# Tiles of normed activations and of the feed-forward's inner values, 32 bytes longer per partition

## The chip, the cores and the metric

The kernel runs on one core of a Trainium2 chip. The metric is the device time of one execution in microseconds. Five engines work side by side and meet at semaphores: TensorE (PE in the rows, with its weight loads as PEld), VectorE (DVE), ScalarE (ACT), GpSimd (POOL) and SyncE (SP, which here only issues transfers).

## What is computed

A two-layer diffusion-style transformer block followed by a second block with a mixer, on one sequence of 512 tokens with 1024 features, all in float32. Cut to the lines that hold nearly all of the arithmetic:

```python
def conv_ffn(hn, win, conv_w, conv_b, wout):      # twice: 1024 -> 2 x 2816 -> 1024
    u = hn @ win
    y = conv_b + sum(up[:, tap:tap + S] * conv_w[tap] for tap in range(3))
    gate, val = jnp.split(y, 2, axis=-1)
    return (jax.nn.silu(gate) * val) @ wout

def swiglu(u, w_gate, w_up, w_down):              # twice: 1024 -> 2 x 2816 -> 1024
    return (jax.nn.silu(u @ w_gate) * (u @ w_up)) @ w_down
...
# between them: attention over chunks with a relative bias (16 heads), latent attention (16 heads),
# and a mixer of differential attention (8 heads) and an mLSTM (4 heads); every branch starts from
# modulate(rms_norm(h)) and ends with h = h + gate * (o @ w_out)
```

## The kernel before

**How a product is made.** Activations lie with features on the 128 partitions and the 512 tokens along the free axis, in tiles of 128 x 512 float32. A product keeps float32's precision by splitting each operand into an upper part H (type float32r) and a remainder L, and by adding three products: H·H, H·L, L·H. `mm3` (L325) issues them on L327, L328 and L329: the weight block (128 x 128) is the stationary operand, the activations (128 x 512) are the moving one, in the order H, L, H. `gemm` (L331) runs `mm3` over the 8 feature tiles: 24 matmuls into one PSUM tile `ps_g`. Weight slabs come by DMA into `wr` and are split by ScalarE (L310) and VectorE (L311) into `wh` and `wl`.

**The tiles that are touched.** `hl` (L343) makes a pair (H, L) of such activations. With the tag `u`, in the pool `gp`, it makes the normed and modulated activations of every branch (8 pairs), the heads' outputs on their way to an output product, and the latents. With the tag `hid`, in the pool `pf`, it makes the inner values of the feed forward. A tag has a fixed number of buffers, which its tiles take in turn: 16 for `u`, 24 for `hid`. In a pool, the buffers of a tag lie one behind the other. Each is 2048 bytes per partition, so in the kernel before all 16 buffers of `u` begin at the same place within 128 bytes. In the built program that place is 64 (the first buffer begins at byte 69312 = 541 x 128 + 64). The weights' buffers `wh` and `wl` (4096 bytes each) all begin at 64, too. The buffers of `hid` begin at 64 in the first convolutional feed forward (where a pool with two tiles of one column is open beneath `pf`), and at 0 in the other three. The tile `xs` (mLSTM's convolved inputs) begins at 0, the tile `yh` (outputs of the differential attention) at 64, the tiles `tw` (weights for the last two row blocks of a branch) at 0 in the first attention and at 64 in the latent attention. The trace shows no addresses: these are read from the built program.

**The order of the work.** The program is one long sequence written out at build time, with the semaphores set from the tiles' uses: attention (to 300 us), first convolutional feed forward (300 to 690), latent attention (690 to 960), second convolutional feed forward (960 to 1340), first gated feed forward (1340 to 1715), mixer (1715 to 2290), second gated feed forward (from 2290). A feed forward runs in three parts of 8, 8 and 4 inner tiles: two `gemm` from `u` for each inner tile, split into `hid`, then 8 output columns from `hid`, `n` inner tiles each. The last two inner tiles are multiplied in halves of 256 tokens (`tail`, L430), so that the next norm can begin on the first half.

Of the kernel before, what the change touches and what calls it, by code (L numbers as in the profile page):

```python
# [31 lines left out]

# ---------------------------------------------------------------- layout

# [35 lines left out]
def _tail(w):  # L70
    """last TAIL row blocks: [2][128][4 column blocks x TAIL x 128]"""
    return _group(_blocks(w[-TAIL * P:]), 4)
# [111 lines left out]

# ---------------------------------------------------------------- device

# [5 lines left out]
class _Norm:  # L192
    """Norm of the residual stream and its modulation, by columns of tokens."""

# [33 lines left out]
class _Norm2(_Norm):  # L228
    """Final norm of the first block (gain g), then the norm that the second block starts with.

    With A the sum of h**2 and B that of (g h)**2 over the D features, the product of the two factors
    (A / D + EPS) ** -0.5 and (B / D / (A / D + EPS) + EPS) ** -0.5 is ((B + EPS A) / D + EPS ** 2) ** -0.5.
    """

# [23 lines left out]
    def finish(self):  # L258
        """the residual stream itself after the first of the two norms"""
        k, nc = self.k, self.k.nc  # L260
        for cs in HALVES:
            k.rsqrt(self.r1, self.sums(cs), D, cs, self.t)
        for j in range(KD):
            h = k.h[j]
            nc.vector.scalar_tensor_tensor(h, h, self.g[:, j:j + 1], self.r1, ALU.mult, ALU.mult)


class _NormOut(_Norm):
    """Final norm, to memory."""

# [13 lines left out]
class _K:  # L284
# [8 lines left out]

    # ---- small helpers
    def col(self, name, j=0, n=1):
# [18 lines left out]
    def stream(self, specs, ahead=1):  # L314
        """wload(*spec) for each, as many ahead of their use"""
        q = [self.wload(*specs.pop(0)) for _ in range(ahead)]

        def take():
            if specs:
                q.append(self.wload(*specs.pop(0)))  # L320
            return q.pop(0)

        return take
# [19 lines left out]
    def hl(self, pool, tag, bufs, src=None):  # L343
        h = pool.tile([P, T], F32R, tag=tag, bufs=bufs, name=tag + "h")
        l = pool.tile([P, T], F32R, tag=tag, bufs=bufs, name=tag + "l")
        if src is not None:
            self.split(src, h, l)
        return h, l
# [4 lines left out]

    # ---- norms: sums of squares over the features, by columns of tokens
    def sq(self, acc, j, src, cs=FULL, scale=1.0, eng=None, first=False):
# [14 lines left out]
    def lnexp(self, ins):  # L370
        """the table set that has both Ln and Exp, loaded behind ins"""
        with self.tc.issue_after(ins.ins):
            self.preload = self.nc.scalar.preload_act_table_set("natural_log_exp_and_others")

    def rsqrt(self, r, ms, dim, cs, tmp, eps=None):
        """r = (ms / dim + EPS) ** -0.5; with eps, that constant (its tile, its value) for EPS"""
        nc = self.nc
        r, t = r[:, cs], tmp[:, cs]
        with self.tc.issue_after(self.preload.ins):
            nc.scalar.activation(r, ms, AF.Ln, bias=eps[0] if eps else self.eps, scale=1.0 / dim)  # L380
            nc.scalar.activation(r, r, AF.Exp, scale=-0.5)
        nc.vector.scalar_tensor_tensor(t, r, -0.5 / dim, r, ALU.mult, ALU.mult)
        nc.vector.scalar_tensor_tensor(t, ms, (eps[1] if eps else EPS) * dim, t, ALU.add, ALU.mult)
        nc.vector.scalar_tensor_tensor(r, t, 1.5, r, ALU.add, ALU.mult)
# [33 lines left out]

    # ---- last products of a branch by halves of the tokens, each followed by its half of the next norm
    def tail_weights(self, pool, tags, wname):  # L420
        """(H, L) for each half of the column blocks"""
        nc = self.nc
        w = [pool.tile([P, 1024], F32R, tag=t, bufs=n, name="tw") for t, n in tags]
        for q in range(2):
            r = self.gp.tile([P, 1024], F32, tag="wr", bufs=4, name="wr")
            nc.sync.dma_start(r, self.a[wname][q])
            self.split(r, w[2 * q], w[2 * q + 1])
        return w
# [17 lines left out]
    def gemm_halves(self, ws, acts):  # L446
        """column blocks ws (H, L) on the first tokens, then on the others"""
        pss = [self.pg() for _ in ws]
# [6 lines left out]

    # ---- modulation vectors: one column of 128 outputs per job
    def gemv(self, j, cact, bias):
# [11 lines left out]

    # ---- attention of one head: softmax per tile of queries, block transposes, values  # L470
    def softmax(self, pool, s, n, add, scale, pn):
        """exp((s+add)*scale - max) and, in st, 1/sum at column 2."""
        nc = self.nc
# [7 lines left out]
    def heads(self, pool, n, begin, lag=2):  # L481
        """n heads, a tile of queries at a time; transposes run lag tiles behind the softmax.

        begin(h) -> probs, v, m, done: probs(i) gives the normalized [128 queries, 128(i+1) keys], v the values
        (H, L), [128 keys, 4, m], done takes the result, [m, 512]."""
        wait = []
# [18 lines left out]
    def transpose(self, i, p, pt):  # L505
        """query tile i of the probabilities into the upper and lower parts, keys on partitions"""
        t = self.pg(tag="t")
# [13 lines left out]
    def stacked(self, src, tiles, keys, scale=1.0):  # L521
        """Rows 64 e on of src as two operands e for products over 128 rows.

        tiles: three; the first two become the operands, with the upper part in rows 64 e on and the lower part
        in the other rows, or for keys the upper part in all; the third gets the lower parts, rows as in src."""
        nc = self.nc
# [9 lines left out]
    def stacked_scores(self, s, q, k, low, e, i, stop=True):  # L536
        """scores of query tile i with the keys up to its end"""
        nc = self.nc
        rs, qs, ks = slice(64 * e, 64 * e + 64), slice(i * P, i * P + P), slice(0, i * P + P)
        nc.tensor.matmul(s, q[:, qs], k[:, ks], start=True, stop=False)  # L540
        nc.tensor.matmul(s, q[rs, qs], low[rs, ks], start=False, stop=stop)  # L541
# [7 lines left out]
    def pair_out(self, pool, dram, p, ps, e):  # L549
        """output of head 2p+e into the rows of its pair; pairs but the last wait in DRAM."""  # L550
        if e == 0:
# [15 lines left out]

    # ---- program
    def build(self):
# [44 lines left out]
    def c_act(self, ca, j):  # L614
        """silu of a row of c on every partition"""
        nc = self.nc
# [21 lines left out]

    # ---- first layer: attention over chunks with relative bias
    def block_a(self, cact, m0):  # L640
# [85 lines left out]
    def branch_out(self, pool, tags, od, w, gate, mk_norm):  # L726
        """product of the heads' outputs with the output weights, into the residual stream"""
        tw = self.tail_weights(pool, tags, w + "t")
# [7 lines left out]

    # ---- feed forward with a causal convolution
    def conv_ffn(self, l, norm, gate, nbg, mk_norm):
# [45 lines left out]

    # ---- second layer: latent attention
    def rope(self, pool, ps, cos, sin):
# [127 lines left out]

    # ---- gated feed forward
    def swiglu(self, n, norm, gt, mk_norm):
# [18 lines left out]

    # ---- second block's mixer
    def mix(self, norm, ada):
# [100 lines left out]
    def ml_gates(self, pp, gps, plc, slr, b):  # L1038
        """gate pre-activations to the exponents of the quadratic form, relative to chunks."""
        nc, a = self.nc, self.a  # L1040
# [52 lines left out]
    def ml_heads(self, pl, u, mg, dram, plc, tri, slr, b):  # L1093
# [7 lines left out]
        def back4(n, h):  # L1101
            """H and L of the two blocks of a head, as split"""
            t = pl.tile([P, 4, T], F32R, tag="xs", bufs=4, name=n)
# [8 lines left out]
        def scores(h):  # L1112
            """weighted scores, keys on partitions: (H, L) of the queries from 128 j on for each tile j of keys"""
            ksl, qsl = back4("mk", h), back4("mq", h)
# [48 lines left out]
        def normed(h, num, den):  # L1163
            """with d the greater of |den| and exp(em), the norm of num / d is
            num * (mean(num ** 2) + EPS * d ** 2) ** -0.5; acc sums to 256 times what is in brackets"""
            em = self.pg()
# [56 lines left out]
    def diff(self, u, px):  # L1223
# [3 lines left out]
        with self.tc.tile_pool(name="pd", bufs=1) as pd:  # L1227
# [11 lines left out]
            nc.scalar.activation(lc[:, 0:2], lc[:, 0:2], AF.Exp)  # L1239
            # -(exp(a) - exp(b) + 0.2)  # L1240
            nc.vector.tensor_tensor(lc[:, 2:3], lc[:, 1:2], lc[:, 0:1], ALU.subtract)
# [94 lines left out]
```

## Time and profile before

| what | value |
|---|---|
| median of the runs shown (2767.37, 2770.97) | 2769.17 us |
| span of the profiled execution | 2771.6 us |
| TensorE busy | 2659.2 us, 96% |
| TensorE weight loads | 2129.6 us, 77% |
| VectorE busy | 1759.9 us, 63% |
| ScalarE busy | 1205.0 us, 43% |
| granted TensorE clock, mean | 0.980 of 2.4 GHz |

The profile has one execution's time, its span; it is 2.4 us over the median of the runs. A matmul's duration in the rows is longer than its share of the engine, because matmuls are pipelined: one is still draining while the next streams. What a matmul costs in a stream is the distance from its start to the next one's start (its pace). The timeline rows give starts with two decimals, so the pace is taken over many matmuls.

### The profile page before, as it was taken

The page shows a single profiled execution, that of the slowest core. Times are in us where ns is not written, and L with a number is a line of the kernel's source. Part 1 is how long each engine was busy: PE and PEld are TensorE (multiplying, and loading weights), DVE is VectorE, ACT ScalarE, POOL GpSimd, SP SyncE. Part 2 cuts the span into 40 slices and gives each one's busy share as a digit, 9 for nine tenths or more (in the row PEclk, how much of TensorE's full clock was granted, in tenths as well). Part 3 has the DMA queues.
Part 4 walks back from the last instruction along what each step waited for, and adds up shares of the span by engine and source line. Part 5 has one row for each costly group of instructions (what it writes and reads, how often), then busy time and mean ns, then how long its engine had stood idle before and what let it go on. Part 6 is the DMA issues. An engine that isn't in the chain of part 4 may idle for free.

```text
span 2771.6 us, 33871 instructions
## 1 busy us (share of the span) xinstructions
PE 2659.2 (96%) x12306; PEld 2129.6 (77%) x12306; DVE 1759.9 (63%) x3349; ACT 1205.0 (43%) x2100; POOL 91.8 (3%) x138
## 2 busy tenths in 40 slices
PE   7999899999899999999899999999999999999997
PEld 5777778788677778878788888777777777788886
DVE  7777896866778896966733335788456456533334
ACT  5565532334567442324522223566446334422222
POOL 1000200000000100000100001000000000100000
PEclk9999999999899999999999999999999999999999
DMA  8664476652143475753133332322247754233331
GB/s 271 188 184 144 145 248 204 223 173 79 43 106 111 139 229 187 252 176 120 54 99 93 98 113 80 92 75 78 72 149 258 239 186 133 77 95 95 99 107 46
DMA packets 138092, 385.24 MB, mean 139 GB/s; under 512 B 22322, under 2 KB 26546, under 8 KB 137924
## 3 DMA queue, kind: packets, MB, share of 16 engines
q1 hardware_dynamic: 137924, 383.06, 43.6%
q8 instruction: 98, 1.61, 0.2%
q14 instruction: 70, 0.57, 0.1%
HBM read 341.05 MB, written 26.21 MB: 133 GB/s over the span
## 4 chain that ended last, share of the span: by engine, by line
PE 33%; issue 13%; DVE 2%; DMA 1%; ACT 1%; POOL 1%; SPq 0%; DVEq 0%; ACTq 0%; POOLq 0%
PE ps_g L329 9%; PE ps_g L327 9%; PE ps_g L328 9%; PE ps_s L541 1%; DMA stg<-xc 1%; PE ps_t L327 1%; PE ps_t L328 1%; PE ps_t L329 1%; PE ps_s L540 0%; PE ps_o L367 0%; POOL ul L400 0%; PE ps_t L509 0%; POOL acc L361 0%; DMA mv<-mv 0%; DVE tn L393 0%
## 5 line engine op out<-in xcount | busy, mean ns | idle before, releaser
L327 PE MATMUL ps_g<-uh,wh 128*128 128x512 f32 (+1 forms) x2244 | 866.2, 389 | 30.7 <-ACT uh L340 11.7
L328 PE MATMUL ps_g<-ul,wh 128*128 128x512 f32 (+1 forms) x2244 | 875.7, 391 | 15.4 <-POOL ul L400 11.9
L329 PE MATMUL ps_g<-uh,wl 128*128 128x512 f32 (+1 forms) x2244 | 868.3, 388 | 1.1 <-DVE wl L311 1.1
L310 ACT CAST wh<-wr 128x1024 fp32r<-128x1024 f32 (+4 forms) x406 | 411.6, 1015 | 990.3 <-PE ps_g L328 730.6
L311 DVE TENSOR_TENSOR wl<-wr,wh 128x1024 fp32r<-128x1024 f32 (+4 forms) x406 | 479.1, 1181 | 284.7 <-ACT wh L310 270.4
L327 PEld LDWEIGHTS ps_g<-uh,wh 128*128 128x128 f32 x2244 | 425.3, 191 | 128.5 <-ACT uh L340 14.3
L328 PEld LDWEIGHTS ps_g<-ul,wh 128*128 128x128 f32 x2244 | 428.3, 191 | 111.5 <-POOL ul L400 20.3
L329 PEld LDWEIGHTS ps_g<-uh,wl 128*128 128x128 f32 x2244 | 428.7, 191 | 89.0 <-DVE wl L311 3.8
L461 DVE CUSTOM_DVE_ANT_0 wr<-wr,cact 128x1024 f32<-128x1024 f32 x184 | 225.8, 1232 | 73.0 <-DMA wr<-mod 72.9
L327 PE MATMUL ps_g<-hidh,wh 128*128 128x512 f32 x640 | 252.9, 395 | 7.8 <-ACT hidh L340 7.8
L329 PE MATMUL ps_g<-hidh,wl 128*128 128x512 f32 x640 | 253.0, 395 | 0.9 <-DVE wl L311 0.9
L328 PE MATMUL ps_g<-hidl,wh 128*128 128x512 f32 x640 | 252.9, 395 | 0.0
L327 PEld LDWEIGHTS ps_g<-hidh,wh 128*128 128x128 f32 x640 | 120.4, 188 | 37.9 <-ACT hidh L340 9.5
L329 PEld LDWEIGHTS ps_g<-hidh,wl 128*128 128x128 f32 x640 | 120.7, 189 | 29.7 <-DVE wl L311 1.3
L328 PEld LDWEIGHTS ps_g<-hidl,wh 128*128 128x128 f32 x640 | 120.7, 189 | 29.1 <-DVE hidl L341 0.6
L444 DVE SCALAR_TENSOR_TENSOR h<-ps_g,mods,h 128x512 f32<-128x512 f32 (+1 forms) x112 | 72.8, 652 | 94.1 <-PE ps_g L329 93.5
L444 DVE SCALAR_TENSOR_TENSOR h<-ps_g,hg,h 128x512 f32<-128x512 f32 (+1 forms) x64 | 43.6, 682 | 134.4 <-PE ps_g L329 134.2
L477 ACT ACTIVATE p<-p,st 128x128 f32<-128x128 f32 (+1 forms) x192 | 107.2, 560 | 30.2 <-DVE st L476 29.2
L929 DVE TENSOR_TENSOR cv<-ps_g,cv 128x512 f32<-128x512 f32 x44 | 30.4, 691 | 137.9 <-PE ps_g L329 137.2
L361 POOL TENSOR_TENSOR acc<-acc,sq 128x256 f32<-128x256 f32 x42 | 35.9, 855 | 2049.0 <-ACT sq L360 1365.7
L340 ACT CAST hidh<-cv 128x512 fp32r<-128x512 f32 x88 | 54.6, 621 | 93.8 <-DVE cv L756 93.8
L340 ACT CAST pth<-ps_t 128x128 fp32r<-128x128 f32 (+3 forms) x160 | 65.7, 424 | 53.7 <-PE ps_t L509 52.5
(362 smaller groups left out, 3607.7 us busy)
## 6 DMA issues: line engine op xcount, KB each, us to landing
wr<-mod SPq DMA_DIRECT2D x184, 512.0 KB, 4.2
wr<-fin SPq DMA_DIRECT2D x88, 512.0 KB, 4.4
wr<-fout SPq DMA_DIRECT2D x40, 512.0 KB, 3.9
wr<-w1g SPq DMA_DIRECT2D x22, 512.0 KB, 3.6
wr<-w1u SPq DMA_DIRECT2D x22, 512.0 KB, 3.6
wr<-w2g SPq DMA_DIRECT2D x22, 512.0 KB, 3.5
wr<-w2u SPq DMA_DIRECT2D x22, 512.0 KB, 3.5
wr<-w1d SPq DMA_DIRECT2D x20, 512.0 KB, 3.6
```

The costliest lines, as they stand in the source:

```text
L310: nc.scalar.copy(h[:, :n], r[:, :n])
L311: nc.vector.tensor_tensor(l[:, :n], r[:, :n], h[:, :n].bitcast(F32), ALU.subtract)
L327: mm(ps, wh, xh, start=start, stop=False)
L328: mm(ps, wh, xl, start=False, stop=False)
L329: mm(ps, wl, xh, start=False, stop=stop)
L340: self.nc.scalar.copy(h, src)
L361: (eng or nc.vector).tensor_tensor(acc[:, cs], acc[:, cs], s[:, cs], ALU.add)
L444: self.nc.vector.scalar_tensor_tensor(self.h[j][:, cs], ps, g, self.h[j][:, cs], ALU.mult, ALU.add)
L461: nc.vector.tensor_tensor_reduce(w, w, cact, 1.0, 0.0, ALU.mult, ALU.add, accum_out=self.mods[:, j:j + 1])
L477: nc.scalar.activation(p[:, :n], p[:, :n], AF.Exp, bias=st[:, 0:1], scale=-1.0, accum_out=st[:, 1:2])
L541: nc.tensor.matmul(s, q[rs, qs], low[rs, ks], start=False, stop=stop)
L929: nc.vector.tensor_tensor(t, pss[1], t, ALU.mult)
```

## The change

Each buffer that `hl` makes for the tags `u` and `hid` becomes 520 columns long instead of 512 (2080 bytes instead of 2048), and the tile that is used is its first 512 columns. The buffers of a tag then begin 32 bytes further on from one to the next, so that within 128 bytes they begin at 64, 96, 0, 32 and so on in turn. Buffers that lie behind move by 16 x 32 = 512 bytes in `gp`, and by 512 bytes or 512 + 24 x 32 = 1280 bytes in the pools above it: `wh`, `wl`, `tw`, `xs` and `yh` keep their place within 128 bytes. The tile `kr` of the latent attention takes a buffer of `u` and so moves to 32.

```diff
     def hl(self, pool, tag, bufs, src=None):
-        h = pool.tile([P, T], F32R, tag=tag, bufs=bufs, name=tag + "h")
-        l = pool.tile([P, T], F32R, tag=tag, bufs=bufs, name=tag + "l")
+        pad = 8 if tag in ("u", "hid") else 0
+        h = pool.tile([P, T + pad], F32R, tag=tag, bufs=bufs, name=tag + "h")[:, :T]
+        l = pool.tile([P, T + pad], F32R, tag=tag, bufs=bufs, name=tag + "l")[:, :T]
         if src is not None:
             self.split(src, h, l)
         return h, l
...
```

The rest of the diff empties comments and docstrings. On every engine the instructions stand in the same order as before, with the same tiles and buffers by number; lines behind `hl` are numbered one higher.

How many matmuls have their moving operand at which place within 128 bytes, counted in the two built programs:

| moving operand, columns | kernel | at 0 | at 32 | at 64 | at 96 |
|---|---|---|---|---|---|
| `u`, 512 | before | 0 | 0 | 6444 | 0 |
| `u`, 512 | after | 1722 | 1482 | 1748 | 1492 |
| `hid`, 512 | before | 1440 | 0 | 480 | 0 |
| `hid`, 512 | after | 512 | 448 | 512 | 448 |
| `u`, 256 | before | 0 | 0 | 768 | 0 |
| `u`, 256 | after | 188 | 196 | 192 | 192 |
| `hid`, 256 | before | 288 | 0 | 96 | 0 |
| `hid`, 256 | after | 64 | 128 | 64 | 128 |

As a stationary operand, `u` stands in 672 matmuls (480 of 256 columns, 192 of 512), at 64 before and spread over the four places after.

## Rows read from the trace of the kernel before

**Rows 1.** The page's head: span, busy time by engine, granted clock in 40 slices.
```profile
span 2771.6 us, 33871 instructions
PE 2659.2 (96%) x12306; PEld 2129.6 (77%) x12306; DVE 1759.9 (63%) x3349; ACT 1205.0 (43%) x2100; POOL 91.8 (3%) x138
PEclk9999999999899999999999999999999999999999
```
**Rows 2.** Lines by form, TensorE: line, engine, operation, out<-in, shapes, count | busy us, mean ns | idle before.
```profile
L327 PE MATMUL ps_g<-uh,wh 128*128 128x512 f32 x2084 | 824.1, 396 | 23.1 <-ACT uh L340 11.7 <-DVE cv L753 4.3 <-DVE mods L462 3.0
L328 PE MATMUL ps_g<-ul,wh 128*128 128x512 f32 x2084 | 822.7, 395 | 2.5 <-DVE ul L341 1.5 <-DVE ul L402 1.0
L329 PE MATMUL ps_g<-hidh,wl 128*128 128x512 f32 x640 | 253.0, 395 | 0.9 <-DVE wl L311 0.9
```
**Rows 3.** Timeline, TensorE, second convolutional feed forward, from `u`: start us, us, instruction.
```profile
999.77 0.39 PE L329 MATMUL ps_g<-uh,wl 128*128 128x512 f32 x1
...
1009.97 0.39 PE L329 MATMUL ps_g<-uh,wl 128*128 128x512 f32 x1
```
**Rows 4.** Timeline, TensorE, first gated feed forward, from `hid`.
```profile
1459.54 0.39 PE L328 MATMUL ps_g<-hidl,wh 128*128 128x512 f32 x1
...
1470.04 0.39 PE L328 MATMUL ps_g<-hidl,wh 128*128 128x512 f32 x1
```
**Rows 5.** Tile `hidh`: duration ns min/median/max, first and last start; one stretch per feed forward.
```profile
L327 PE MATMUL ps_g<-hidh,wh x64: 389/389/500, 403.9 to 449.7; 128*128 128x512 f32 x64
...
L327 PE MATMUL ps_g<-hidh,wh x64: 393/394/499, 1054.4 to 1099.3; 128*128 128x512 f32 x64
...
L327 PE MATMUL ps_g<-hidh,wh x64: 394/394/394, 1443.2 to 1487.3; 128*128 128x512 f32 x64
...
L327 PE MATMUL ps_g<-hidh,wh x64: 394/394/395, 2478.6 to 2522.7; 128*128 128x512 f32 x64
```
**Rows 6.** The same view of the tiles `xs`, `yh` and, in one stretch, `uh`.
```profile
L328 PE MATMUL ps_g<-xs,wh x48: 388/394/398, 2051.4 to 2122.3; 128*128 128x512 f32 x48
...
L328 PE MATMUL ps_g<-yh,wh x64: 389/389/628, 1944.4 to 2033.6; 128*128 128x512 f32 x64
...
L327 PE MATMUL ps_g<-uh,wh x89: 389/389/390, 989.8 to 1049.6; 128*128 128x512 f32 x89
```
**Rows 7.** Timeline, TensorE, first convolutional feed forward, `hid` after a stop.
```profile
411.86 0.50 PE L327 MATMUL ps_g<-hidh,wh 128*128 128x512 f32 x1 [1.31 <-ACT hidh L340]
412.19 0.40 PE L329 MATMUL ps_g<-hidh,wl 128*128 128x512 f32 x1
...
413.85 0.39 PE L328 MATMUL ps_g<-hidl,wh 128*128 128x512 f32 x1
...
415.89 0.39 PE L328 MATMUL ps_g<-hidl,wh 128*128 128x512 f32 x1
```
**Rows 8.** Timeline, TensorE, tails of 256 columns, from `u` with `tw`.
```profile
286.75 0.28 PE L327 MATMUL ps_g<-uh,tw 128*128 128x256 f32 x1
...
290.05 0.28 PE L328 MATMUL ps_t<-ul,tw 128*128 128x256 f32 x1
...
296.07 0.28 PE L327 MATMUL ps_g<-uh,tw 128*128 128x256 f32 x1
...
298.68 0.28 PE L329 MATMUL ps_g<-uh,tw 128*128 128x256 f32 x1
...
941.73 0.28 PE L327 MATMUL ps_g<-uh,tw 128*128 128x256 f32 x1
...
945.09 0.28 PE L328 MATMUL ps_t<-ul,tw 128*128 128x256 f32 x1
```
**Rows 9.** Windows: stretch, length, busy us (instructions) by engine, granted clock, DMA share, GB/s.
```profile
90.00:300.00 210.00, 205.90 (x1023) 154.53 (x1023) 165.67 (x474) 123.63 (x288) 9.32 (x24) 0.99 0.56 172
...
690.00:960.00 270.00, 252.12 (x1261) 190.44 (x1260) 209.03 (x540) 168.44 (x380) 13.45 (x16) 0.93 0.35 99
960.00:1054.00 94.00, 88.53 (x416) 72.73 (x416) 87.49 (x160) 44.81 (x65) 6.73 (x7) 0.99 0.69 224
1443.00:1488.00 45.00, 45.00 (x194) 36.08 (x193) 16.36 (x17) 8.96 (x10) 0.00 (x0) 1.00 0.31 94
...
1715.00:2287.00 572.00, 552.73 (x2602) 433.38 (x2600) 359.82 (x750) 302.91 (x569) 10.43 (x17) 0.98 0.44 141
```

## The prediction

> **What bounds the kernel now.** I read the page's head first: of a span of 2771.6 us TensorE is busy 96% of the time, VectorE 63%, ScalarE 43%, at a clock that is granted nearly everywhere in full, which is 2.4 GHz [rows 1]. So TensorE's pace is the kernel's pace, except where it stands still for others. The lines by form say which matmuls these are: the three lines of `mm3` on `u` (2084 each with `ps_g`) and on `hid` (640 each) [rows 2]. In them it hardly waits: 2.5 us over 2084 matmuls on L328. In the windows of the products from `hid` it is busy without a gap (45.00 of 45 us) [rows 9].
>
> Then the timeline, for what one matmul costs. From `u` the starts run from 999.77 to 1009.97 us over 45 steps: 10.20 / 45 = 226.7 ns each [rows 3]. From `hid` in the first gated feed forward: 1459.54 to 1470.04 over 45 steps, 233.3 ns each [rows 4]. 512 columns at 2.4 GHz are 213.3 ns, so each matmul pays 13.4 or 20.0 ns on top. Both paces are constant over long stretches. What tells the two apart? The view of `hidh` has four stretches of the same 64 matmuls: the median is 389 ns in the first and 394 in the other three [rows 5]. The first and the second are the same code with other weights; what differs is where `hid` begins, at 64 or at 0. `xs` at 0 takes 394, `yh` and `uh` at 64 take 389 [rows 6]. The weights begin at 64 in all of these. So a moving operand that begins at the weights' place costs 226.7 ns, and one that begins 64 bytes off costs 233.3.
>
> **The change, part by part.** No instruction is added, removed or moved on any engine or queue, and no wait. Only addresses change, so every term is a number of matmuls times a change of pace.
>
> (a) `u`, 512 columns, 6444 matmuls, all at 226.7 now. 1748 stay at 64: nothing. 1722 go to 0: 1722 x 6.67 ns = +11.5 us.
>
> (b) `hid`, 512 columns. Now 1440 at 0 pay 1440 x 6.67 = 9.6 us over the better pace; afterwards 512 do, 3.4 us: -6.2 us.
>
> (c) Places 32 and 96 take 1482 + 1492 + 448 + 448 = 3870 matmuls. No moving operand stands there before, so this is bounded, not read. Call d the difference to 226.7 ns. From below: the tails with 256 columns show that the same addresses can run at two paces. From 286.75 to 290.05 there are 28 steps of 117.9 ns, from 296.07 to 298.68 23 steps of 113.5 ns, and with weights and `u` both at 64 there are 28 steps of 120.0 ns from 941.73 to 945.09 [rows 8]. 256 columns are 106.7 ns, so the surcharge can fall to 6.8 ns; on 512 columns that is 220.1, d = -6.6. From above: after a stop a stream needs some matmuls to find its pace. In the first one from `hid` at 64 seven steps from 412.19 to 413.85 take 237 ns each, the next nine to 415.89 take 226.7 [rows 7]. A stream whose places alternate might never settle: d = +10.5, and then the places 0 and 64 pay it too. Between them I take 233.3, d = +6.6, the pace of operands that are not at the weights' place: that is what the nearest row shows for "off by some bytes", and it also lies in the middle of settled and unsettled streams. 3870 x 6.67 = +25.8 us.
>
> (d) 256 columns: 644 matmuls go to 32 or 96; at -6.6 to +6.7 ns each that is -4 to +4 us. `hid` against `tw` at other places gains up to 1 us, `u` as a stationary operand (672 matmuls) moves by less than 4 us either way, `kr` has 64 matmuls. I take +1 us for all.
>
> (e) What is hidden. 1884 of the matmuls in (a) and (c) stand in the attentions and the mixer (384 + 156 + 1344), where TensorE is busy only 205.90 of 210, 252.12 of 270 and 552.73 of 572 us [rows 9], since it waits for softmax and transposes there. Their mean rise is (1722 + 2974) x 6.67 / 6444 = 4.86 ns, 9.2 us together. I take a third as hidden: -3.1 us. In the feed forwards nothing hides: VectorE is close behind TensorE where the modulation vectors are computed alongside (87.49 us of 94) [rows 9], so a slower TensorE still sets the end there, and a faster one would gain little.
>
> (f) The writers (ScalarE, VectorE, GpSimd on `u` and `hid`) and the small transfers from `u` in the latent attention: no instruction more, and covered by TensorE's stream. Without that cover, ten nanoseconds on a few hundred instructions would be some 3 us.
>
> Sum: 11.5 - 6.2 + 25.8 + 1 - 3.1 = +29 us, on the profiled 2771.6 us 2800.6; this execution is 2.4 us over the median of the runs (2769.2), so about 2798 us, +1.0%.
>
> [...] The rows show that a matmul's time depends on where its moving operand begins: 389 against 394 ns for the same code [rows 5]. [...]
>
> **Rivals.**
> - *The place doesn't matter* (the two paces have another cause, such as the weights' addresses or the stage): 0 us, 2769. For it: no row varies the place alone. Against it: six stretches of four tiles, all sorted by place [rows 5, 6].
> - *32 and 96 run like 64* (d about 0, say because operands are read in pieces of 64 bytes and only whole pieces count): 11.5 - 6.2 = +5, so 2774.
> - *The other side: faster.* If the surcharge comes from two streams of reads in step with each other, places in between could take it away: d = -6.6, 5.3 - 25.5 = -20, 2749. For it: the 113.5 ns in the tail [rows 8]. Against: in 6444 + 1920 matmuls of 512 columns no stretch runs at 220. It decides once d is under -1.4 ns (5.3 / 3870), at places 32 and 96.
> - *Never settled.* Each step has another place than the one before, and all run at the 237 ns of a fresh stream: 6444 x 10.4 = 67 us; `hid`, whose mean is now 231.7, 1920 x 5.4 = 10 us; a third of 1884 x 10.4 = 20 us hidden, -6.5: +71, 2840. It passes 2% (+55 us) once the mean pace of all is above 235 ns.
>
> **How the numbers follow.** Forecast (d near +6.6, 2798, own range 2785 to 2812): 0.42. Like 64: 0.22. Faster: 0.12. Never settled: 0.17. Place without effect: 0.07. The range for 8 in 10 goes from the faster case, 2748, to just short of the unsettled one, 2836. A change of 2%, 55 us, is about what a measurement of this kernel can tell from no change. Faster by that much would need d = -15 ns or so, below the 213.3 ns of the columns themselves: 0.02. Slower by over 2% is most of the unsettled case: 0.14. Within 2%: 0.84.
>
> **What would show it.** In the trace of the changed kernel: instruction counts and order as before; the timeline from `u` in a feed forward with steps that vary by operand (226.7 at 64, 233.3 at 0, and the open ones at 32 and 96), with a mean near 231.6 where it is 226.7 now; the four stretches of `hidh` alike in their median, where now one differs from three; the feed forwards' hidden stages longer by 2%, the stages from `hid` about the same. The prediction is wrong if the steps from `u` stay at one pace (place without effect), if operands at 32 and 96 run at 227 or less, or if operands at 64 lose their 226.7 in mixed company.

## The result, and the profile after

The changed kernel takes 2789.91 us (2788.51 and 2791.3), the kernel before 2769.17: a ratio of 1.0074 with a 95% interval of 1.0050 to 1.0098, 20.7 us more. I forecast 2798, with 2785 to 2812 as that case's own range.

Page head of the kernel after, to be held against [rows 1]: span, busy time and count by engine, granted clock.
```profile
span 2789.5 us, 33871 instructions
PE 2682.2 (96%) x12306; PEld 2126.3 (76%) x12306; DVE 1761.3 (63%) x3349; ACT 1206.2 (43%) x2100; POOL 91.8 (3%) x138
PEclk9999999999999999999999999999999989999999
```
The counts are the same on every engine. The span is 17.9 us longer and TensorE is busy 23.0 us longer, at a mean granted clock of 0.981 where it was 0.980; VectorE and ScalarE do the same work in 1.4 and 1.2 us more. Lines by form, TensorE, kernel after [rows 2]:
```profile
L327 PE MATMUL ps_g<-uh,wh 128*128 128x512 f32 x2084 | 833.2, 400 | 20.5 <-ACT uh L340 10.7 <-DVE cv L754 4.3 <-ACT et L1170 2.4
L328 PE MATMUL ps_g<-ul,wh 128*128 128x512 f32 x2084 | 828.7, 398 | 2.5 <-DVE ul L341 1.5 <-DVE ul L403 1.0
L329 PE MATMUL ps_g<-hidh,wl 128*128 128x512 f32 x640 | 252.6, 395 | 0.1
```
The matmuls from `u` went from 395 or 396 to 398 or 400 ns, those from `hid` stayed at 395. The timeline of the stretch from `u` in the second convolutional feed forward [rows 3], kernel after:
```profile
999.80 0.40 PE L327 MATMUL ps_g<-uh,wh 128*128 128x512 f32 x1
...
1001.67 0.39 PE L329 MATMUL ps_g<-uh,wl 128*128 128x512 f32 x1
...
1003.03 0.40 PE L329 MATMUL ps_g<-uh,wl 128*128 128x512 f32 x1
...
1004.89 0.39 PE L328 MATMUL ps_g<-ul,wh 128*128 128x512 f32 x1
...
1006.07 0.39 PE L327 MATMUL ps_g<-uh,wh 128*128 128x512 f32 x1
...
1010.21 0.40 PE L327 MATMUL ps_g<-uh,wh 128*128 128x512 f32 x1
```
45 steps take 10.41 us, 231.3 ns each, where they took 226.7. They are not even: the six from 1001.67 to 1003.03 take 226.7 ns each, the five from 1004.89 to 1006.07 take 236. Over all matmuls of 512 columns from `u` the mean pace is 231.5 ns. Tile `hidh`, the stretches that answer to [rows 5]: duration ns min/median/max, first and last start.
```profile
L327 PE MATMUL ps_g<-hidh,wh x64: 389/394/502, 403.1 to 448.8; 128*128 128x512 f32 x64
...
L327 PE MATMUL ps_g<-hidh,wh x64: 389/394/422, 1054.6 to 1098.5; 128*128 128x512 f32 x64
...
L327 PE MATMUL ps_g<-hidh,wh x64: 393/394/399, 1444.3 to 1488.1; 128*128 128x512 f32 x64
...
L327 PE MATMUL ps_g<-hidh,wh x64: 393/394/399, 2493.4 to 2537.2; 128*128 128x512 f32 x64
```
All four now have a median of 394, where the first had 389.

**Where the 17.9 us lie.** I took the start of the same matmul in both traces at the stage boundaries, and split each stage's TensorE time into the pace of the steps under 250 ns (512 columns) and the rest. The mixer is taken to the end of its last output product at 2382.7 us: the section on the order of the work has the second gated feed forward begin at 2290, but its first matmul starts at 2383.60 us, and the products between belong to the mixer.

| stage | length before, us | change | from the pace |
|---|---|---|---|
| attention | 297.8 | -0.6 | +2.6 |
| first convolutional feed forward | 389.1 | +1.3 | +7.0 |
| latent attention | 269.9 | -1.7 | +1.2 |
| second convolutional feed forward | 380.6 | +0.6 | +3.8 |
| first gated feed forward | 374.4 | +4.0 | +4.0 |
| mixer | 667.7 | +9.6 | +5.2 |
| second gated feed forward | 379.0 | +4.2 | +4.1 |

The pace costs 27.9 us in all. In the gated feed forwards all of it arrives at the end; in the convolutional ones 1.9 of 10.8 us do in this pair of traces. Windows of the first convolutional, the first gated feed forward and the mixer up to its last products, kernel after (columns as in [rows 9]), and then the first two of the kernel before:
```profile
300.00:690.80 390.80, 378.10 (x1690) 306.58 (x1691) 295.49 (x489) 150.47 (x208) 12.63 (x15) 0.99 0.53 177
1340.00:1719.00 379.00, 372.01 (x1660) 302.47 (x1661) 159.28 (x202) 115.58 (x164) 10.92 (x14) 0.99 0.29 92
1719.00:2299.00 580.00, 561.72 (x2598) 436.18 (x2596) 359.88 (x749) 303.41 (x569) 10.45 (x17) 0.97 0.43 139
```
```profile
300.00:690.00 390.00, 375.75 (x1690) 310.22 (x1691) 295.60 (x490) 150.40 (x208) 12.94 (x16) 0.98 0.54 178
1340.00:1715.00 375.00, 368.10 (x1659) 302.30 (x1658) 159.10 (x201) 115.89 (x164) 10.89 (x14) 0.99 0.30 93
```
The same 1690 matmuls of the first convolutional feed forward keep TensorE busy 2.35 us longer in a window that is 0.8 us longer. Its stops (steps of over 450 ns, counted as what they take beyond a step of 226.7) fall from 12.2 to 10.9 us, and matmuls at a granted clock of 0.50 (steps of 400 to 450 ns) cost 1.8 us over full pace in place of 4.4. I read this as a slower TensorE leaving VectorE time; one pair of traces does not show it, and the part on term (e) below takes more of them. In the gated one TensorE hardly stops (6.9 of 375 us idle before, 7.0 of 379 after).

### The profile page after: what moved, and what is told of

It is laid out like the page before. It is cut to its first block, busy times and chain, and to the rows that moved or that the text cites. A ratio compares the mean times of both kernels' runs of the same rounds, so it can differ in the third digit from the quotient of the medians.

```text
span 2789.5 us, 33871 instructions
## 1 busy us (share of the span) xinstructions
PE 2682.2 (96%) x12306; PEld 2126.3 (76%) x12306; DVE 1761.3 (63%) x3349; ACT 1206.2 (43%) x2100; POOL 91.8 (3%) x138
## 4 chain that ended last, share of the span: by engine, by line
PE 33%; issue 13%; DVE 2%; ACT 1%; DMA 1%; POOL 1%; SPq 0%; DVEq 0%; ACTq 0%; POOLq 0%
PE ps_g L327 9%; PE ps_g L329 9%; PE ps_g L328 9%; PE ps_s L542 1%; PE ps_t L327 1%; PE ps_t L328 1%; PE ps_t L329 1%; PE ps_o L368 0%; PE ps_s L541 0%; DMA stg<-xc 0%; POOL ul L401 0%; PE ps_t L510 0%; POOL acc L362 0%; DMA mv<-mv 0%; DVE tn L394 0%
## 5 line engine op out<-in xcount | busy, mean ns | idle before, releaser
L327 PE MATMUL ps_g<-uh,wh 128*128 128x512 f32 (+1 forms) x2244 | 874.0, 393 | 28.1 <-ACT uh L340 10.7
```

What stands on the lines that cost most here:

```text
L327: mm(ps, wh, xh, start=start, stop=False)
```

## The experiments

All edits are against the kernel before, so `hl` makes tiles of 512 columns. "Place" is where a buffer begins; "distance" is the place of the moving operand minus that of the weights, in the built program. `hl`'s buffers are shifted by tiles that nobody uses, as in

```diff
+        if ahead and new:
+            pool.tile([P, ahead], F32, tag=tag + "ahead", name=tag + "ahead")
         h = pool.tile([P, T + pad], F32R, tag=tag, bufs=bufs, name=tag + "h")[:, :T]
+        if ahead and new:
+            pool.tile([P, 32 - ahead], F32, tag=tag + "behind", name=tag + "behind")
...
```

Here `pad` is 0 and `new` is true at a tag's first use in a pool. The two tiles together are 32 columns, 128 bytes: what lies behind the buffers, the weights behind `u` above all, moves by 128 bytes, so its place within 128 stays, but the distance modulo 256 changes.

**Every place by itself.** Three kernels hold all buffers of a tag at one place: `ahead` is 8 and 16 columns for `u` and `hid` in u96_hid64, 16 and 8 in u0_hid32, 24 and 24 in u32_hid96.

> All buffers of u begin at 96 (one place, 2048 bytes apart as before), those of hid 64 bytes further on: at 0 in the first feed forward, at 64 in the other three; weights stay at 64. Theory 'settling' (a stream settles on a constant pace when all its moving operands begin at one place, and never settles when the places differ): the steps from u are constant to 1 ns, at a value between 220 and 240 ns that no row has shown yet; hid turns round, 233.3 ns in the first feed forward and 226.7 in the other three, -6.4 us in all. Rival 'spacing' (it is the 2080 bytes between buffers that unsettle the stream, not the place): u keeps 226.7 ns, total 2763. Rival 'dear places' (32 and 96 cost more by themselves): u varies from step to step and means 232 or more, total over 2795.

> All buffers of u begin at 0, those of hid at 96 in the first feed forward and at 32 in the other three; weights at 64. Settling: u constant at 233.3 ns as hid was at 0 before, 6444 x 6.6 ns = +43 us less some 4 us hidden, total about 2808 plus what hid does at 32 (constant, unknown, +-13 us). Spacing: 226.7 ns from u, 2769. Dear places: u at 233.3, hid at 32 varying with a mean of 232 or more.

> All buffers of u begin at 32, those of hid at 32 in the first feed forward and at 96 in the other three; weights at 64. Settling: constant paces for both, of a value that is read here for 32 (u and the first feed forward's hid must agree) and that agrees for 96 with the run that has u there. Spacing: 226.7 ns, 2769. Dear places: varying steps, mean 232 or more, total over 2795.

Measured: 2797.92, 2795.84 and 2793.73 us beside 2772.25; ratios 1.0088 (1.0056 to 1.0121), 1.0081 (1.0052 to 1.0110), 1.0073 (1.0044 to 1.0102). Timeline from `u`, second convolutional feed forward, u96_hid64:
```profile
1000.12 0.40 PE L328 MATMUL ps_g<-uh,wh 128*128 128x512 f32 x1
...
1009.96 0.40 PE L328 MATMUL ps_g<-uh,wh 128*128 128x512 f32 x1
```
and u0_hid32:
```profile
1000.28 0.39 PE L330 MATMUL ps_g<-uh,wl 128*128 128x512 f32 x1
...
1010.08 0.39 PE L330 MATMUL ps_g<-uh,wl 128*128 128x512 f32 x1
```
and u32_hid96:
```profile
999.88 0.40 PE L330 MATMUL ps_g<-uh,wl 128*128 128x512 f32 x1
...
1009.68 0.40 PE L330 MATMUL ps_g<-uh,wl 128*128 128x512 f32 x1
```
42 steps each: 234.3, 233.3 and 233.3 ns. So alternating places are not needed for a loss: `u` at each of the other three places has a slower pace than the mix (231.5), and the guess d = +6.6 for 32 and 96 (+6.6 and +7.6) holds. `hid` in u96_hid64, now at 64 in the last three feed forwards, runs at 226.7, and in the other two kernels at 233.3. Two expectations were missed: `hid` at 0 in the first feed forward of u96_hid64 ran at 228.9 and not at 233.3, a first sign that the place within 128 bytes is not all; and u0_hid32 ended at 2795.84 us where some 2808 were expected, with `u` at the expected pace (term (e) below).

**Only the weights moved.** w0 leaves `u` where it is, and `hid` at its places within 128 bytes, and moves `wh` and `wl` from 64 to 0, by 16 columns ahead of them.

> Only the weights' buffers move, from 64 to 0; u stays at 64, hid at 64 in the first feed forward and 0 in the others. If it is the distance between the moving operand's place and the weights' that sets the pace: u 233.3 ns, hid 226.7 in the last three feed forwards and 233.3 in the first, +43 - 4 - 6 = about +33 us, 2802. If it is the moving operand's own place: all paces as before, 2769.

Measured: 2785.98 beside 2772.25, ratio 1.0051 (1.0028 to 1.0074). Tile `hidh`, second convolutional and second gated feed forward, w0:
```profile
L334 PE MATMUL ps_g<-hidh,wh x60: 389/389/398, 1061.2 to 1101.5; 128*128 128x512 f32 x60
...
L334 PE MATMUL ps_g<-hidh,wh x64: 389/389/398, 2495.3 to 2538.2; 128*128 128x512 f32 x64
```
`hid` at 0 has the 389 ns that it had only at 64 [rows 5], and `u`, unmoved at 64, now takes 233.3 ns a step. It is not the operand's own place that sets the pace, but its distance to the weights. The paces came as expected, but the time was 16 us under the 2802 that I had added up from them.

**Each tag alone.** u_alone lengthens only the tiles of `u`, hid_alone only those of `hid`.

> The change for u alone (2080 bytes per buffer), hid as before. Theory 'difference' (226.7 ns only where the moving operand begins at the weights' place within 128 bytes and its neighbours do too; 233.3 at any other one place; 231.5 in mixed company): u at 231.5, hid as before, 6444 x 4.5 ns less some hidden, +20 to +26 us: the whole effect of the change. Rival 'both halves' (hid gives a part): +10 to +15.

> The change for hid alone, u as before. Difference: hid in the first feed forward from 226.7 to 231.5 (480 x +4.8 ns = +2.3 us), in the other three from 233.3 to 231.5 (1440 x -1.8 = -2.6 us): 0 us, within 2 us. Both halves: +5 to +10.

Measured, beside 2770.31: 2785.36, ratio 1.0053 (1.0014 to 1.0092), with `u` at 231.5 ns; and 2771.88, ratio 1.0005 (0.9994 to 1.0017), with `hid` at 231.9 (231.8 in the kernel before, as a mean of 226.7 and 233.3). The loss is `u`'s. The +15.1 us of u_alone are under the +20 to +26 expected, and the rival *both halves* forecast +10 to +15 for it; but that rival needs +5 to +10 from hid_alone, whose interval, -1.7 to +4.7 us, leaves them out. The two differences, 15.1 and 1.6 us, make 16.7 of the change's 20.7, which their intervals allow.

**How fine, how far.** hid_space128 sets the buffers of `hid` 2176 bytes apart, so that their place within 128 bytes is the same while within 256 it alternates; the distance within 128 is 0, 0, +4 and -4 in the four feed forwards. hid_fine does the same with +8, +16, -16 and -8.

> The buffers of hid are 2176 bytes long (128 more), so all of a feed forward begin at one place within 128 bytes again, and the tile lies at an offset in its buffer that differs by feed forward: 0, 16, 17 and 15 columns, which makes its distance to the weights' place 0, 0, +4 and -4 bytes (within 128). Difference: 226.7 ns in the first two feed forwards, so the buffers' spacing and their distance over 256 bytes count for nothing; at +4 and -4 bytes 226.7 if the place counts in pieces of some bytes, else 233. Rival 'spacing': varying steps with a mean of 231 in all four. u is as before.

> As hid_space128, with distances of +8, +16, -16 and -8 bytes between hid and the weights in the four feed forwards. Difference in steps of 32 bytes: 226.7 or 233.3 in each, by the 32-byte piece it begins in (+8 and +16 at 226.7, -16 and -8 at 233 or the like). Difference by bytes: paces that go from 226.7 to 233.3 with the distance, or a pace under 226.7 at one of them, which would make a faster kernel.

Measured, in one run each: 2767.05 and 2767.77 us beside 2770.31. The streams of the feed forwards' first parts run at 233.3, 228.9, 237.8 and 228.9 ns, in hid_fine at 233.3, 231.1, 231.1 and 231.2. None reaches 226.7 where places alternate by 128, so "the same within 128 bytes" is not enough. The first two streams of hid_space128 have the same distances modulo 256 and two paces, 42 steps each:
```profile
429.62 0.39 PE L331 MATMUL ps_g<-hidh,wl 128*128 128x512 f32 x1
...
439.42 0.39 PE L331 MATMUL ps_g<-hidh,wl 128*128 128x512 f32 x1
...
1069.87 0.39 PE L331 MATMUL ps_g<-hidh,wl 128*128 128x512 f32 x1
...
1079.48 0.39 PE L331 MATMUL ps_g<-hidh,wl 128*128 128x512 f32 x1
```
They are 233.3 and 228.8 ns.

So in the scans every distance was constant for a whole feed forward: `wh` and `wl` are the halves of one tile, and shift in it from feed forward to feed forward (by 64, 32, 96, 124 columns in scan_far; 4, 1, 127, 112 in scan_near).

```diff
-        h = self.gp.tile([P, 1024], F32R, tag="wh", bufs=3, name="wh")
-        l = self.gp.tile([P, 1024], F32R, tag="wl", bufs=3, name="wl")
+        w = self.gp.tile([P, 2176], F32R, tag="wh", bufs=3, name="wh")
+        h, l = [w[:, self.off + q:self.off + q + 1024] for q in (0, 1024)]
```

> The weights' pair lies at an offset in a longer buffer, which differs by feed forward, so that the distance from the weights' place to the moving operand's, within 512 bytes, is for u 256, 384, 128 and 16 in the four feed forwards and for hid 256, 320, 64 and 464; in the attentions and the mixer it stays 0. Theory 'same place within 128 bytes': 226.7 ns from u at 256, 384 and 128. Theory 'same place within 256': 226.7 at 256 alone. Theory 'same place within 512': 226.7 at none of these, 229 to 234 at all, and hid at 64 between 228.9 and 233.3 as it was in the run w0. Each distance is constant in its stage, so each pace should settle.

> As scan_far, with distances for u of 496 (-16), 508 (-4), +4 and +64 in the four feed forwards and for hid of 496 (-16), 444, 452 and 0. If only the exact same place settles at 226.7: u at 229 to 238 in all four, hid 226.7 in the last feed forward alone. If a whole 16-byte or 32-byte piece counts: u at +4 at 226.7. If a pace under 226.7 exists near it (u at 220 or so at -4 or -16), a faster kernel can be made of it.

Measured: 2761.25 and 2761.89 beside 2770.52. Timelines from `u`, 42 steps each; scan_far at a distance of 256, then of 128:
```profile
460.15 0.39 PE L331 MATMUL ps_g<-uh,wh 128*128 128x512 f32 x1
...
469.67 0.39 PE L331 MATMUL ps_g<-uh,wh 128*128 128x512 f32 x1
...
1500.13 0.39 PE L330 MATMUL ps_g<-ul,wh 128*128 128x512 f32 x1
...
1509.89 0.39 PE L330 MATMUL ps_g<-ul,wh 128*128 128x512 f32 x1
```
scan_near at -16, +4 and +64:
```profile
460.14 0.39 PE L330 MATMUL ps_g<-ul,wh 128*128 128x512 f32 x1
...
469.94 0.39 PE L330 MATMUL ps_g<-ul,wh 128*128 128x512 f32 x1
...
1500.22 0.39 PE L329 MATMUL ps_g<-uh,wh 128*128 128x512 f32 x1
...
1509.74 0.39 PE L329 MATMUL ps_g<-uh,wh 128*128 128x512 f32 x1
...
2530.24 0.39 PE L330 MATMUL ps_g<-ul,wh 128*128 128x512 f32 x1
...
2539.86 0.39 PE L330 MATMUL ps_g<-ul,wh 128*128 128x512 f32 x1
```
They give 226.7 and 232.4, then 233.3, 226.7 and 229.0 ns. Settled streams from all these kernels, by distance modulo 256 bytes:

| distance | ns a step | distance | ns a step |
|---|---|---|---|
| 0, 256 | 226.7 | 128 | 232.4, 233.3 |
| +4 | 226.7 | 160 (-96) | 234.3 |
| +16 | 226.7 or 228.3 | 188 to 208 | 233.3 |
| +32 | 233.3 | 224, 240 | 233.3 |
| +64 | 228.9 (once 233.3) | 252 (-4) | 232.4 |
| +96 | 233.3 | | |

Both signs of a distance are not alike: +64 gives 228.9, -64 (192) gives 233.3. In the kernel before, `u` is at 0 in this table and `hid` at 0 once and at 192 three times.

**A kernel with all distances 0, and one with fewer stops.** same_place shifts `hid` by 16 columns in the last three feed forwards and `xs` by 16 (80 columns ahead of it); same_place_pair also makes `wh` and `wl` the halves of one tile of 2048 columns.

> The edit: buffers of u and hid 2048 bytes again; the buffers of hid in the last three feed forwards are moved by 64 bytes and xs by 64, so that every moving operand of 512 columns that u, hid and xs give begins at the place of its weights modulo 256 bytes. Theory 'same place within 256': hid goes from 233.3 to 226.7 ns in three feed forwards (1440 x 6.6 = -9.5 us) and xs from 229-233 to 226.7 (192 matmuls, about -0.9 us): 2759 to 2760 where the kernel before takes 2769 to 2770, ratio 0.996. Rival 'place only as in the kernel before' (hid at 64 loses elsewhere, or VectorE sets the end of these stages): less than 3 us.

> The edit: same_place, and the two halves of the split weights (wh, wl) are one tile of 2048 columns with three buffers, in place of two tiles of 1024 with three buffers each; addresses modulo 256 bytes stay the same, as does the count of matmuls. scan_far and scan_near, which had that tile, ended at 2761 and 2762 us though several of their stages ran at 228 to 234 ns. Theory 'one tile helps by itself' (fewer buffers to wait for and to hand out, earlier start of the first streams): 8 to 15 us under same_place, 2745 to 2752. Rival 'the scans were faster by their distances alone': the same as same_place within 2 us.

Measured: 2759.91 beside 2772.09, ratio 0.9965 (0.9950 to 0.9981), and 2744.88, ratio 0.9908 (0.9894 to 0.9923). Tile `hidh`, the two gated feed forwards, same_place:
```profile
L328 PE MATMUL ps_g<-hidh,wh x64: 389/389/389, 1437.9 to 1480.7; 128*128 128x512 f32 x64
...
L328 PE MATMUL ps_g<-hidh,wh x63: 389/389/389, 2470.1 to 2512.3; 128*128 128x512 f32 x63
```
The gain of 12 us is the forecast 10 and some: the gated feed forwards are 3.3 and 3.6 us shorter than before, the second convolutional one 2.2, and the stages whose pace is as before moved by up to 3.5 us either way. The runs of same_place lay between 2752.8 and 2775.4 us and the mean granted clock at these ends was 0.985 and 0.976; those of the pair lay between 2742.5 and 2746.2.

The pair's 15 us more are not pace (226.9 ns in the mean in both) but stops: in the two traces, TensorE's stops between products of 512 columns come to 89.3 and 76.0 us over full pace, the steps of 400 to 450 ns behind them to 30.0 and 26.1. ScalarE's waits show what moved; same_place:
```profile
ACT wh L311 <- PE ps_g L329: 725.3, 229, 6.3
```
and same_place_pair (us in total, times, longest):
```profile
ACT wh L311 <- PE ps_g L330: 428.5, 122, 4.4
ACT cv L939 <- PE ps_g L330: 155.8, 42, 4.4
```
ScalarE's split of the next weights waits for TensorE to free their buffer. In the pair it stands later in ScalarE's row, behind the instruction that takes the finished product from PSUM (L539), and no longer holds that one up. In the first attention, ScalarE's timeline in same_place and then in same_place_pair:
```profile
73.30 1.05 ACT L311 CAST wh<-wr 128x1024 fp32r<-128x1024 f32 x1 [2.71 <-PE ps_g L329]
74.25 0.59 ACT L539 ACTIVATE q<-ps_g 128x512 fp32r<-128x512 f32 x1
...
72.55 0.60 ACT L539 ACTIVATE q<-ps_g 128x512 fp32r<-128x512 f32 x1 [2.93 <-PE ps_g L330]
73.04 1.04 ACT L311 CAST wh<-wr 128x1024 fp32r<-128x1024 f32 x1
```
This fits with how the scans, which have the one tile for the weights too, could be 9 us faster than before with slower streams. That the order alone does it, rather than the number of buffers, was not tried.

## Why the prediction was right, and where it was not

**The bound held in part.** TensorE's pace is the kernel's pace where it hardly stops: 27.9 us of slower steps became 17.9 us of span, whole in the gated feed forwards, less than half in the convolutional ones (term (e)). And the 9.6 us of slow `hid` steps that I had priced from [rows 4] came back when same_place took them away (12 us).

**Terms (a) and (c): the sum right, the parts wrong.** I priced `u` at 11.5 us for place 0 and 2974 x 6.67 = 19.8 us for 32 and 96, 31.3 us or a mean of 231.6 ns. Measured are 231.5; in the kernel before the mean is 227.2, not 226.7, since steps behind a stop are slow there, too (237 ns in [rows 7]), so the rise is 27.8 us. But the steps don't sort by place: in the changed kernel, with the buffers' addresses from the built program, those from `u` take between 231 and 232.4 ns at each of the four places. The 1748 at 64, which I held at 226.7, lost over 4 ns each, and those at 0 ran some 2 ns better than 233.3. That is what I had written would make the prediction wrong. Uniform places would have paid my prices (233.3, 233.3, 234.3 for 0, 32, 96, in three kernels); in a mix a step also depends on its neighbours: over some 7700 steps from `u` and `hid` the own distance modulo 256 explains a few per cent of the variance at most, together with those of the step before and the step after more than a third. That the two means, 231.6 and 231.5, agree is then luck: the mix of four places within 128 bytes, eight within 256, has a mean of its own.

The 213.3 ns for 512 columns and the 106.7 for 256, 2.4 columns a nanosecond, can be read in the traces, which give the clock as a share of full speed. At a granted clock of 0.50 six steps of 512 columns from `u` take 426.7 ns each, twice 213.3; and at 1.00, with operand and weights both at 64, steps of 512 and of 256 columns are 226.7 - 120.0 = 106.7 ns apart [rows 3, 8]. Window (columns as in [rows 9]) and timeline, kernel before:
```profile
330.51:333.90 3.39, 3.39 (x9) 2.65 (x10) 2.06 (x4) 2.60 (x4) 0.00 (x0) 0.50 0.13 53
```
```profile
330.84 0.63 PE L328 MATMUL ps_g<-ul,wh 128*128 128x512 f32 x1
...
333.40 0.63 PE L328 MATMUL ps_g<-ul,wh 128*128 128x512 f32 x1
```

**The reading of [rows 5, 6] was half right.** "At the weights' place" was the right reading of 226.7, but I let it stand as a property of a place within 128 bytes. It takes the distance to the weights (w0), modulo 256 (hid_space128, scan_far). The change, therefore, had nothing to find: `u` stood at the best distance already, and no distance tried is under 226.7 ns. That also settles the rival *faster*: d was +6.6 and +7.6.

**Term (b) and `hid`.** I had -6.2 for it and, in (c), 896 x 6.67 = +6.0 for its places 32 and 96, together nothing. Measured: 231.8 before and after, and hid_alone 1.0005. The four stretches became alike at 394, not at a mix of 389 and 394, again since the steps don't sort by place.

**Term (e) is the one that was mis-sized.** I let 3.1 us be hidden, all of it in the attentions and the mixer, and nothing in the feed forwards. Part of that is a count: 2412 of the 512-column matmuls from `u` stand in the attentions and the mixer (528 + 396 + 1488), not 1884, so that a third of their rise would have been 3.9 us. The larger part is "in the feed forwards nothing hides", which fails in the convolutional ones. The one trace of the kernel before is a poor yardstick for them: in hid_alone, hid_space128, hid_fine and same_place, where `u` keeps its pace, the convolutional feed forwards are 1.7 to 4.8 us shorter than in it beyond what the pace of `hid` makes. So the six kernels with a slower `u` are set here against the mean of those five traces. Each entry is what the stages grew by, of what their pace would add, in us:

| kernel | convolutional feed forwards | gated feed forwards | mixer | attentions |
|---|---|---|---|---|
| the change | 5.0 of 10.8 | 8.2 of 8.1 | 10.7 of 5.2 | -2.2 of 3.7 |
| u_alone | 3.8 of 9.4 | 9.4 of 9.3 | 6.3 of 5.1 | -3.0 of 3.7 |
| u0_hid32 | 8.9 of 15.6 | 13.2 of 13.0 | 4.0 of 8.0 | 2.4 of 4.2 |
| u32_hid96 | 4.3 of 15.7 | 13.1 of 13.0 | 4.5 of 7.8 | 1.5 of 4.9 |
| u96_hid64 | 6.9 of 12.5 | 8.7 of 8.7 | 8.7 of 9.0 | 1.4 of 5.5 |
| w0 | 4.0 of 11.3 | 6.8 of 6.8 | 6.8 of 7.6 | 4.9 of 4.2 |
| sum | 32.9 of 75.3 | 59.4 of 58.9 | 41.0 of 42.7 | 5.0 of 26.2 |

Outside the gated feed forwards the five traces differ among themselves by some 4 to 7 us, so the sums say more than an entry. The gated feed forwards pass on all of a slower pace and the mixer nearly all; the attentions hide four fifths and the convolutional feed forwards over half. The third that I let the attentions and the mixer hide together is what they hid (46.0 of 68.9 arrive); what I put at nothing in the convolutional feed forwards is 5.8 us in the change. As I read the windows, TensorE there waits at the start of a stream for what VectorE and ScalarE make, and a slower TensorE finds more of it ready: in the first convolutional feed forward its stops come to 7.8 to 10.9 us in these six kernels and to 11.4 to 12.2 in the five others. That is the sign to expect, but no run changed VectorE's work alone. I had read 87.49 of 94 us busy [rows 9] as "VectorE close behind"; it says as well that part of a slower TensorE costs nothing. Of the 8.3 us by which the forecast was over (29 against 20.7), the base of 227.2 makes 3.5 and this term about 3: the change's row adds up to 21.7 of 27.8, 6.1 hidden and not 3.1. What is left is within what two runs a side can vary. The term is also why u0_hid32 and w0 ended below what was expected of them.

**Terms (d) and (f).** All products that are not of 512 columns take 494 us in place of 497, with the waits behind them, inside the -4 to +4 that I gave; VectorE and ScalarE are at 1761.3 and 1206.2 us, 1.4 and 1.2 more.

**The rivals.** *The place doesn't matter* is refuted by same_place, where the weights stay, `hid` moves, and its steps go from 233.3 to 226.7; but the cause that this rival named, the weights' addresses, is half of the true one: in w0 the same instructions, with the weights moved by 64 bytes, take `u` from 226.7 to 233.3. (The stretches of [rows 5, 6] that I counted against it are seven, not six, and `xs`, 388 to 398 ns, is not one settled pace.) The weights' address alone is worth 0.5% of the kernel's time (w0, 2785.98 beside 2772.25 us). *Like 64* fell with 233.3 and 234.3 at 32 and 96. *Never settled* was right in kind, wrong in price: the mix runs at 231.5, not at the 237 of a fresh stream [rows 7]. Those 237 ns are one pattern of several that a stream can hold (one stretch of hid_space128 stays at 237.8 throughout), and no upper price for a mix.

## What to carry to other kernels

When one matmul form runs at two paces in one trace, list the addresses of both its operands before pricing a move: what counted here was the distance between moving operand and weights, and it showed only when the weights alone were moved (w0, 226.7 to 233.3 ns). Give all buffers of a stream one distance, and the good one: rotating through places made 231.5 ns a step of 226.7. And where an engine's pace gets worse, look stage by stage at who starts the products: stages in which TensorE waits for another engine gave part of the loss back (32.9 of 75.3 us arrived in the convolutional feed forwards, 59.4 of 58.9 in the gated ones).

## What the runs showed of the hardware that was not expected

- A 128 x 512 matmul in float32r costs 226.7 ns a step where its moving operand and its weights lie 0 or 4 bytes apart modulo 256, 228.3 or 228.9 at some other distances, and 232.4 to 234.3 at most; in the stretches of [rows 3, 4] the granted clock was 1.00. Why is open: the runs show paces and addresses, and no cause.
- A stream can hold one of several paces at the same distances (233.3 and 228.9 in hid_space128, 226.7 and 228.3 at +16 in scan_far), each constant over many matmuls; what picks one was not found.
- One short stop cost more than its length. In same_place TensorE waits 2.37 us before a matmul from `hid` at 548.90, and 1.1 us later comes this window (columns as in [rows 9]):
```profile
549.96:553.31 3.35, 3.35 (x9) 2.60 (x8) 1.90 (x2) 1.05 (x1) 0.00 (x0) 0.51 0.00 0
```
The granted clock is 0.51. The eight matmuls that begin there take 3.35 us where eight steps of 226.7 ns are 1.81: 1.5 us on top of the stop. The window before the stop, 540 to 546 us, had a granted clock of 1.00.
